# Sample attention with each lot of cache products in one run, zero-padded new values and four cache buffers

## The chip, the core and the metric

The kernel runs on one core of one Trainium2 chip. The metric is the device time of one execution in microseconds (us); a kernel's time is the median over its runs. TensorE is called PE below, VectorE DVE, ScalarE ACT, GpSimd POOL, and SyncE, which issues nearly all DMAs, SP.

## What is computed

The reference is one step of a decoder layer for a prompt of 1024 tokens and for 8 samples of 8 new tokens each. Cut to what matters here, the samples' attention is:

```python
def dilated_group_sample(q, kk, vv, window, dilation):   # kk, vv: cache rows, then the new rows
    idx = (L + jnp.arange(T))[:, None] - dilation * jnp.arange(n_neigh + 1)[None, :]
    kg, vg = kk[:, idx], vv[:, idx]
    s = jnp.einsum('bthd,btjhd->bthj', q, kg) * SCALE
    s = jnp.where(valid[None, :, None, :], s, NEG_INF)
    return softmax_attend(s, vg, 'bthj,btjhd->bthd')
# three (window, dilation) groups, merged by their softmax denominators
```

Around it stand a norm and an input projection with a convolution branch, the prompt's own dilated attention, an output projection, a gated feed-forward block with a short convolution, and a last norm.

## The kernel before, in words

All tokens (1024 of the prompt and 64 of the samples) go through the projections together, as 128-row tiles of features by 1088 tokens. The twelve heads are handled as six pairs p = 0 to 5. `project(p, ...)` makes q, k and v of a pair with three `gemm` calls (lines 184 to 186, three fp32r products each, evicted by DVE at line 447); `sample_attention(p, ...)` is the samples' attention of the pair; `prompt_heads` is the prompt's.

Sample attention runs for p = 0, 1, 2 in a first stage, between the projections (zone "S", from about 99 to 229 us of the profile), and for p = 3, 4, 5 in a second stage, among the prompt's heads and the first part of the output projection (zone "U", from about 395 to 524 us). After that come the rest of the output projection and the feed-forward block, which the change doesn't touch.

In one pair, the 8 samples form four column groups j of 32 rows, and the samples of one group are two halves g = 0, 1. The cache keeps 768 positions, cut in two lots c of 384. So there are four key tiles (g, c) and four value tiles (g, c), each 128 x 1536 numbers (768 KB), which `load_cache` (line 168) brings into a rotation of buffers named "cr": three of them before.

- Scores (line 544): for each lot c, for each g, one key tile is asked for and four products are made, one for each j. Their output is 32 rows high, so that four stand side by side in the array (the profile shows such a product as 128*32). The 64 new keys are one more product in the second lot (line 537, 128*128).
- DVE adds the mask and takes the minimum (line 546), ACT takes the exponential (549), PE turns the weights round in seven transposes (556), the last of which is 64 columns wide, and ACT copies them out in three pieces (558).
- Weighted values (lines 563 and 570): for each g, first the new tokens' values, four products with 64 rows (64*32), then for each c one value tile and 3 x 4 products (128*32). Each fp32 product is two PE instructions in the trace.
- ACT scales the result (572), PE turns it back (575), and DVE puts it in place (582).

The program is written without an order of its own: a framework puts every instruction into its engine's queue by a simulated timeline and by priorities (`tc.high_priority`, `tc.issue_after`), when the kernel is built. Each engine then works through its queue strictly in that order, and an instruction that has to wait holds up what is queued behind it. The products on 32 rows were scheduled one by one, so that other work stands between those of one lot.

Of the kernel before, what the change touches and what calls it, by code (L numbers as in the profile page):

```python
# [20 lines left out]
AF = mybir.ActivationFunctionType  # L21
# [3 lines left out]
P = 128  # L25
D = 1024
S = 1024
B = 8
T = 8
NS = B * T  # L30
# [8 lines left out]
NKEY = NCACHE + NS  # L39
# [7 lines left out]
CH = 384  # L47
NCH = NCACHE // CH
# [32 lines left out]
def trunk_kernel(tc, xT, w_in, w_out, w_gate, w_up, w_down, par, kc, vc, sa, sf, pmask, smask,  # L81
                 yT, kT, vT, ca, cas, cf):
    nc = tc.nc
    with (
# [34 lines left out]
        def zt(z, tag, bufs, s, w=N, dt=F32):  # L119
            return zone[z].tile([P, w], dt, tag=tag, name=nm(s), bufs=bufs)  # L120
# [8 lines left out]
        ident = cp.tile([P, P], F32, name="ident")  # L129
# [295 lines left out]
        def project(p, pump):  # L425
# [39 lines left out]
            def sample_part(c):  # L465
                if c < 2:
                    nc.scalar.activation(new[:, c * NS:(c + 1) * NS], xs[c][:, S:N], AF.Copy,
                                         scale=(1.0 if c else -0.125))
                else:
                    pt = bank(*gbank[0])  # L470
                    nc.tensor.transpose(pt[:NS, :P], xs[c][:, S:N], ident)
                    nc.scalar.activation(vn, pt[:NS, :P], AF.Copy)

            def prompt_part(c):
                x = xs[c]
# [38 lines left out]
        def sample_attention(p, Z, masks):  # L514
            mask, z = masks
            SB, PB = SBUFS[Z][1:]
# [10 lines left out]
                    nc.vector.tensor_copy(zg[g][r, :].rearrange("p (j c) -> p j c", c=32)[:, :, o:o + T],  # L527
                                          src.rearrange("p (j g t) -> p g j t", g=2, t=T)[:, g])
            st = sp.tile([P, 4], F32, tag="sst", name=nm("sst"), bufs=2)
            y = zt(Z, "S", SB, "sy", NKEY)  # L530
            for c in range(NCH):
                ps = bank(Z, "ss", PB)
                n = CH
                first = None
                if c == NCH - 1:
                    n += NS
                    first = nc.tensor.matmul(ps[:, CH:n], za, new[:, NS:], start=True, stop=True)
                for g in range(2):
                    t = load_cache(Z, kc[p, g, c])
                    for j in range(4):  # L540
                        with ExitStack() as order:
                            if first:
                                order.enter_context(tc.issue_after(first.ins))
                            nc.tensor.matmul(ps[32 * j:32 * j + 32, :CH], zg[g][:, 32 * j:32 * j + 32], t[:, j],
                                             start=(g == 0), stop=(g == 1))
# [3 lines left out]
            nc.scalar.activation(y, y, AF.Exp, bias=st[:, 1:2], scale=-1.0, accum_out=st[:, 2:3])  # L549
            nc.vector.reciprocal(st[:, 3:4], st[:, 2:3])  # L550
            pT = zt(Z, "S", SB, "spt", 7 * P)
            for k0, nk in ((0, 4), (4, 3)):
                pt = bank(Z, "ss", PB)
                for k in range(nk):
                    n = min(P, NKEY - (k0 + k) * P)
                    nc.tensor.transpose(pt[:n, k * P:(k + 1) * P], y[:, (k0 + k) * P:(k0 + k) * P + n], ident)
                for (a, e, n) in ([(0, 4, P)] if k0 == 0 else [(0, 2, P), (2, 3, NS)]):
                    nc.scalar.activation(pT[:n, (k0 + a) * P:(k0 + e) * P], pt[:n, a * P:e * P], AF.Copy)
            o2 = zt(Z, "S", SB, "so", 2 * P)
            for g in range(2):  # L560
                po = bank(Z, "ss", PB)
                for j in range(4):
                    nc.tensor.matmul(po[32 * j:32 * j + 32, :P], pT[:NS, 6 * P + 32 * j:6 * P + 32 * j + 32], vn,
                                     start=True, stop=False)
                for c in range(NCH):
                    t = load_cache(Z, vc[p, g, c])
                    for k in range(CH // P):
                        i = CH // P * c + k
                        for j in range(4):
                            nc.tensor.matmul(po[32 * j:32 * j + 32, :P], pT[:, i * P + 32 * j:i * P + 32 * j + 32],  # L570
                                             t[:, j, k * P:(k + 1) * P], start=False, stop=(i == 5))
# [248 lines left out]
        i = 0  # L820
# [818 lines left out]
```

## Time and profile before

| what | value |
|---|---|
| time, median of 3 runs | 1341.75 us (1339.65 to 1345.99) |
| the profiled execution: its own time / span of the profile | 1339.82 us / 1338.0 us |
| PE busy | 97% of the span |
| DVE, ACT, POOL busy | 70%, 42%, 36% |
| mean DMA rate over the span | 157 GB/s |

The profile is one execution. A view of the profile groups instructions by line and tile; the timeline gives start, length and, in brackets, the idle time of the engine ahead of an instruction and what ended it. Matmuls overlap, so their lengths add up to more than the time they take, and what one of them costs PE is read from start to next start.

### The profile page before, as it was taken

To read this page: it belongs to the slowest core of one execution; us is meant where nothing else is said; L and a number is where in the kernel's file an instruction comes from. 1 tells how busy PE (TensorE), PEld (TensorE's weight loads), DVE (VectorE), ACT (ScalarE), POOL (GpSimd) and SP (SyncE) were. 2 spreads that over 40 slices of the span, in tenths; PEclk is the share of its full clock that TensorE was granted. 3 is DMA by queue.
4 is the path that set the end of the run, shared out by engine and by line. 5 is a ranking of instruction groups with operands and counts; after the bars stand their busy time and mean duration, and the time that the engine had idled before them with its cause. 6 is when DMAs were issued, how large, how long until landed. Compare 5 with 4: busy or idle time off the path is not lost.

```text
span 1338.0 us, 25862 instructions
## 1 busy us (share of the span) xinstructions
PE 1297.1 (97%) x10275; PEld 1245.7 (93%) x10275; DVE 937.9 (70%) x1789; ACT 559.8 (42%) x1128; POOL 477.0 (36%) x375
## 2 busy tenths in 40 slices
PE   7999999999999999988999999999999999999996
PEld 7998988999978887888999999999999999999996
DVE  6379779656666657688976676676766669867656
ACT  6312222256674556445633233332333335334432
POOL 1311211211101103430756456564565534444710
PEclk9999999999999999999999999999999999999999
DMA  8147675955689889262033231332213296352412
GB/s 290 56 128 260 234 275 179 242 163 135 206 249 273 270 261 255 90 219 80 2 122 122 91 109 46 122 122 91 99 56 122 76 337 234 108 178 93 156 40 96
DMA packets 92762, 210.27 MB, mean 157 GB/s; under 512 B 13793, under 2 KB 42721, under 8 KB 92641
## 3 DMA queue, kind: packets, MB, share of 16 engines
q1 hardware_dynamic: 92640, 208.62, 48.1%
q8 instruction: 81, 1.33, 0.4%
q14 instruction: 41, 0.33, 0.1%
HBM read 152.55 MB, written 56.04 MB: 156 GB/s over the span
## 4 chain that ended last, share of the span: by engine, by line
PE 56%; DVE 3%; issue 1%; ACT 0%; DMA 0%; DVEq 0%; ACTq 0%
PE g L918 5%; PE g L919 5%; PE g L916 5%; PE py L918 5%; PE py L916 4%; PE py L919 4%; PE px L916 3%; PE pz L918 3%; PE px L919 3%; PE pz L919 3%; PE pz L916 3%; PE px L918 3%; PE g L1490 1%; PE g L1491 1%; PE g L1492 1%; DVE sq L1073 1%
## 5 line engine op out<-in xcount | busy, mean ns | idle before, releaser
L160 POOL TENSOR_TENSOR wl<-wr,wh 128x1024 fp32r<-128x1024 f32 (+1 forms) x36 | 66.9, 1858 | 320.0 <-PE g L186 279.7
L184 PE MATMUL g<-xh,wh 128*128 128x384 f32 (+1 forms) x472 | 158.3, 335 | 0.6 <-DVE qkv L447 0.6
L186 PE MATMUL g<-xh,wl 128*128 128x384 f32 (+1 forms) x472 | 157.1, 333 | 0.0
L185 PE MATMUL g<-xl,wh 128*128 128x384 f32 (+1 forms) x472 | 156.8, 332 | 0.0
L919 PE MATMUL g<-ux,as 128*128 128x272 f32 x504 | 145.1, 288 | 0.0
L918 PE MATMUL g<-ux,as 128*128 128x272 f32 x504 | 144.8, 287 | 0.0
L916 PE MATMUL g<-ux,as 128*128 128x272 f32 x504 | 144.8, 287 | 0.0
L1021 POOL TENSOR_TENSOR wb<-wr,wb 128x512 fp32r<-128x512 f32 x84 | 122.8, 1474 | 49.6 <-ACT wb L1020 49.6
L1373 POOL TENSOR_TENSOR as<-ar,as 128x640 fp32r<-128x640 f32 (+1 forms) x56 | 91.5, 1646 | 100.8 <-ACT as L1372 89.1
L1020 ACT ACTIVATE wb<-wr 128x512 fp32r<-128x512 f32 x84 | 52.5, 629 | 160.7 <-DVE wr L1037 101.8
L692 ACT ACTIVATE y<-y,m 128x128 f32<-128x128 f32 (+1 forms) x192 | 88.7, 467 | 26.9 <-DVE m L680 16.7
L916 PEld LDWEIGHTS g<-ux,as 128*128 128x128 f32 x504 | 95.0, 189 | 0.0
L919 PEld LDWEIGHTS g<-ux,as 128*128 128x128 f32 x504 | 94.8, 188 | 0.0
L918 PEld LDWEIGHTS g<-ux,as 128*128 128x128 f32 x504 | 94.7, 188 | 0.0
L1243 DVE SCALAR_TENSOR_TENSOR fc<-gb,prm,fc 128x1104 f32<-128x1104 f32 x44 | 83.4, 1914 | 14.8 <-ACT fc L1241 14.5
L1021 POOL TENSOR_TENSOR wa<-wr,wa 128x512 fp32r<-128x512 f32 x42 | 57.6, 1375 | 97.5 <-ACT wa L1020 73.6
L184 PEld LDWEIGHTS g<-xh,wh 128*128 128x128 f32 x472 | 89.4, 189 | 3.0 <-issue 1.6
L186 PEld LDWEIGHTS g<-xh,wl 128*128 128x128 f32 x472 | 89.3, 189 | 2.2 <-issue 2.1
L185 PEld LDWEIGHTS g<-xl,wh 128*128 128x128 f32 x472 | 89.5, 190 | 0.6 <-issue 0.2
L655 DVE CUSTOM_DVE_ANT_0 y<-s,pmk 128x128 f32<-128x128 f32 (+1 forms) x192 | 63.5, 379 | 37.0 <-PE s L651 34.5
L397 DVE SCALAR_TENSOR_TENSOR cacc<-gp,prm,cacc 128x1024 f32<-128x1024 f32 x60 | 86.8, 1447 | 0.0
L1463 DVE TENSOR_TENSOR x<-g,x 128x544 f32<-128x544 f32 x76 | 52.5, 717 | 32.9 <-PE g L919 32.9
(370 smaller groups left out, 4244.1 us busy)
## 6 DMA issues: line engine op xcount, KB each, us to landing
cr<-in_kc SPq DMA_DIRECT2D x24, 768.0 KB, 7.9
cr<-in_vc SPq DMA_DIRECT2D x24, 768.0 KB, 6.8
ux<-ub SPq DMA_DIRECT2D x63, 272.0 KB, 4.4
kk<-dk SPq DMA_DIRECT2D x48, 256.0 KB, 6.8
wr<-in_w_gate SPq DMA_DIRECT2D x22, 512.0 KB, 3.3
wr<-in_w_up SPq DMA_DIRECT2D x22, 512.0 KB, 4.4
wr<-in_w_in SPq DMA_DIRECT2D x20, 512.0 KB, 5.5
ub<-u SPq DMA_DIRECT2D x18, 544.0 KB, 4.0
```

The costliest lines, as they stand in the source:

```text
L160: lo_eng.tensor_sub(lo, raw, hi.bitcast(F32))
L184: nc.tensor.matmul(ps[c], whi[:, k, :], xh[:, t0:t0 + n], start=(k == 0), stop=False)
L185: nc.tensor.matmul(ps[c], whi[:, k, :], xl[:, t0:t0 + n], start=False, stop=False)
L186: nc.tensor.matmul(ps[c], wlo[:, k, :], xh[:, t0:t0 + n], start=False, stop=(k == nk - 1))
L397: eng.scalar_tensor_tensor(acc[:, :S], gp[:, j:j + S], col(w0 + j), acc[:, :S], op0=ALU.mult, op1=ALU.add)
L692: nc.scalar.activation(y, y, AF.Exp, bias=m[:, 4 * g + i:4 * g + i + 1], scale=-1.0, accum_out=den[:, g, 2 * hd + u, i:i + 1])
L916: nc.tensor.matmul(ps, whi[:, k, :], xh[:, t], start=(start and k == 0), stop=False, skip_group_check=True)
L918: nc.tensor.matmul(ps, whi[:, k, :], xl[:, t], start=False, stop=False, skip_group_check=True)
L919: nc.tensor.matmul(ps, wlo[:, k, :], xh[:, t], start=False, stop=(k == nk - 1), skip_group_check=True)
L1021: nc.gpsimd.tensor_sub(lo, x, hi.bitcast(F32))
L1243: nc.vector.scalar_tensor_tensor(c[:, :W], gb[i][:, t:t + W], col(C_FW + 3 * f + t), c[:, :W], op0=ALU.mult, op1=ALU.add)
L1373: nc.gpsimd.tensor_sub(lo, raw, hi.bitcast(F32))
```

## The change

The number of cache buffers goes from three to four in both zones. Both tiles that a lot needs are asked for ahead of its products. The products of a lot then carry a high priority and are written in an order in which the tile that was asked for last is used first: for the scores g = 1 and then g = 0; for the values, positions 3, 4, 5, then the new tokens, then 0, 1, 2. The new tokens' values are padded with zero rows from 64 to 128 (a memset of `vn` on POOL), and so are the weights (`y` is 896 wide, with its last 64 columns set to zero on POOL), so that these products have the same shape as the others, the last transpose is full, and ACT copies in two pieces instead of three. The line numbers of the changed kernel differ a little: the scores are line 544 again, the transposes 555, the weighted values 566, the memsets 435 and 532.

```diff
-SBUFS = {"S": (3, 3, 2), "U": (3, 3, 1)}
+SBUFS = {"S": (4, 3, 2), "U": (4, 3, 1)}
...
-            vn = vn[:NS, :]
+            nc.gpsimd.memset(vn[NS:, :], 0.0)
...
-            y = zt(Z, "S", SB, "sy", NKEY)
+            y = zt(Z, "S", SB, "sy", 7 * P)
+            nc.gpsimd.memset(y[:, NKEY:], 0.0)
...
-                for g in range(2):
-                    t = load_cache(Z, kc[p, g, c])
-                    for j in range(4):
-                        with ExitStack() as order:
-                            if first:
-                                order.enter_context(tc.issue_after(first.ins))
-                            nc.tensor.matmul(ps[32 * j:32 * j + 32, :CH], zg[g][:, 32 * j:32 * j + 32], t[:, j],
-                                             start=(g == 0), stop=(g == 1))
+                tiles = [load_cache(Z, kc[p, g, c]) for g in range(2)]
+                with tc.high_priority(offset=AHEAD), tc.issue_after(first.ins) if first else nullcontext():
+                    for g in (1, 0):
+                        for j in range(4):
+                            nc.tensor.matmul(ps[32 * j:32 * j + 32, :CH], zg[g][:, 32 * j:32 * j + 32], tiles[g][:, j],
+                                             start=(g == 1), stop=(g == 0))
...
                 for k in range(nk):
-                    n = min(P, NKEY - (k0 + k) * P)
-                    nc.tensor.transpose(pt[:n, k * P:(k + 1) * P], y[:, (k0 + k) * P:(k0 + k) * P + n], ident)
-                for (a, e, n) in ([(0, 4, P)] if k0 == 0 else [(0, 2, P), (2, 3, NS)]):
-                    nc.scalar.activation(pT[:n, (k0 + a) * P:(k0 + e) * P], pt[:n, a * P:e * P], AF.Copy)
+                    nc.tensor.transpose(pt[:, k * P:(k + 1) * P], y[:, (k0 + k) * P:(k0 + k + 1) * P], ident)
+                nc.scalar.activation(pT[:, k0 * P:(k0 + nk) * P], pt[:, :nk * P], AF.Copy)
...
-                for j in range(4):
-                    nc.tensor.matmul(po[32 * j:32 * j + 32, :P], pT[:NS, 6 * P + 32 * j:6 * P + 32 * j + 32], vn,
-                                     start=True, stop=False)
-                for c in range(NCH):
-                    t = load_cache(Z, vc[p, g, c])
-                    for k in range(CH // P):
-                        i = CH // P * c + k
+                tiles = [load_cache(Z, vc[p, g, c]) for c in range(NCH)]
+                jobs = [(CH // P * c + k, tiles[c][:, :, k * P:(k + 1) * P]) for c in range(NCH) for k in range(CH // P)]
+                jobs.append((6, vn[:, None].to_broadcast([P, 4, P])))
+                with tc.high_priority(offset=AHEAD):
+                    for n, (i, v) in enumerate(jobs[3:] + jobs[:3]):
                         for j in range(4):
                             nc.tensor.matmul(po[32 * j:32 * j + 32, :P], pT[:, i * P + 32 * j:i * P + 32 * j + 32],
-                                             t[:, j, k * P:(k + 1) * P], start=False, stop=(i == 5))
+                                             v[:, j], start=(n == 0), stop=(n == 6))
```

What this does to the order on the engines is seen at three places. The first is PE in stage S, at the weighted values of the first pair. "ss" is the PSUM bank, "cr" a cache tile, "vn" the new tokens' values, "spt" the turned weights, "g" a product of the projection. Before:

```order
L185 MATMUL g_1176<-xl_169,wh_1063 128x384
L186 MATMUL g_1176<-xh_168,wl_1065 128x384
L563 MATMUL ss_978<-vn_619,spt_964 32x128 x4
L570 MATMUL ss_978<-cr_983,spt_964 32x128 x12
L570 MATMUL ss_978<-cr_997,spt_964 32x128 x12
L563 MATMUL ss_1012<-vn_619,spt_964 32x128 x4
L570 MATMUL ss_1012<-cr_1017,spt_964 32x128 x12
L184 MATMUL g_1176<-xh_172,wh_1063 128x384
```

The fourth tile's products (cr_1031) stand 42 rows further down, behind forty projection products and a transpose, in a run of their own. Now, at the same place:

```order
L185 MATMUL g_1133<-xh_132,wh_1058 128x320
L186 MATMUL g_1133<-xl_133,wh_1058 128x320
L566 MATMUL ss_979<-cr_982,spt_966 32x128 x3
L566 MATMUL ss_1013<-cr_1016,spt_966 32x128
L566 MATMUL ss_979<-cr_982,spt_966 32x128
L566 MATMUL ss_1013<-cr_1016,spt_966 32x128
L566 MATMUL ss_979<-cr_982,spt_966 32x128
```

The run goes on like this for 47 more rows: all 56 products of both halves g stand in it, with no projection product between them. As both halves have the same priority, their products alternate, one of bank ss_979 and one of bank ss_1013, the second three behind the first.

The second place is PE in stage U, at the weighted values of the second half of pair p = 3. "s", "t" and "o" are tiles of the prompt's attention. Before:

```order
L563 MATMUL ss_4726<-vn_2001,spt_4678 32x128 x4
L570 MATMUL ss_4726<-cr_4731,spt_4678 32x128
L651 MATMUL s_4233<-kk_3926,qw_3924 128x256
L651 MATMUL s_4233<-kk_3929,qw_3924 128x256
L651 MATMUL s_4233<-kk_3926,qw_3924 128x256
L651 MATMUL s_4233<-kk_3929,qw_3924 128x256
L570 MATMUL ss_4726<-cr_4731,spt_4678 32x128 x6
L719 MATMUL t_4270<-ident,y_4126 128x128
```

Now, with the last projection product ahead and a transpose of the prompt behind:

```order
L186 MATMUL g_6063<-ml_4638,wh_6036 128x320
L187 MATMUL g_6063<-mh_4637,wl_6038 128x320
L566 MATMUL ss_4732<-cr_4735,spt_4685 32x128 x12
L566 MATMUL ss_4732<-vn_2004,spt_4685 32x128 x4
L566 MATMUL ss_4732<-cr_4733,spt_4685 32x128 x12
L752 MATMUL t_4014<-ident,db_4012 128x128 x4
```

What was cut into five runs is one. Not every lot of stage U is whole: at three places an "o" group of the prompt, which has the same priority, still stands inside a values run.

The third place is SP at the start of stage U: "smk" is the mask, "qs" and "kk" are the prompt's queries and keys, "mx" an input of the output projection. Before:

```order
L509 DMA smk_4635<-in_smask 128x832
L168 DMA cr_4648<-in_kc 128x1536
L596 DMA qs_3719<-dq_1997 64x1024 x2
L604 DMA kk_3926<-dk_1998 64x1024 x2
L604 DMA kk_3929<-dk_1998 64x1024 x2
L168 DMA cr_4654<-in_kc 128x1536
L168 DMA cr_4663<-in_kc 128x1536
L268 DMA mx_6268<-mixed_85 128x1088
L168 DMA cr_4669<-in_kc 128x1536
```

Now:

```order
L510 DMA smk_4641<-in_smask 128x832
L169 DMA cr_4655<-in_kc 128x1536
L169 DMA cr_4657<-in_kc 128x1536
L169 DMA cr_4670<-in_kc 128x1536
L169 DMA cr_4672<-in_kc 128x1536
L592 DMA qs_3724<-dq_2000 64x1024 x2
L600 DMA kk_3931<-dk_2001 64x1024 x2
L600 DMA kk_3934<-dk_2001 64x1024 x2
```

All four key tiles of the pair are asked for in a row, ahead of the prompt's queries and keys.

More of the change, by code (lines that the diff above doesn't have):

```diff
@@ L53 @@
 AHEAD = 4000
-SBUFS = {"S": (3, 3, 2), "U": (3, 3, 1)}
+AHEAD = 4000
+SBUFS = {"S": (4, 3, 2), "U": (4, 3, 1)}
 NS1, PN = 3, 4
@@ L471, in sample_part @@
                     nc.tensor.transpose(pt[:NS, :P], xs[c][:, S:N], ident)
-                    nc.scalar.activation(vn, pt[:NS, :P], AF.Copy)
+                    nc.scalar.activation(vn[:NS, :], pt[:NS, :P], AF.Copy)
             def prompt_part(c):
@@ L548, in sample_attention @@
                                                scalar=(st[:, 0:1] if c else 3e38), accum_out=st[:, c:c + 1])
-            nc.scalar.activation(y, y, AF.Exp, bias=st[:, 1:2], scale=-1.0, accum_out=st[:, 2:3])
+            nc.scalar.activation(y[:, :NKEY], y[:, :NKEY], AF.Exp, bias=st[:, 1:2], scale=-1.0, accum_out=st[:, 2:3])
             nc.vector.reciprocal(st[:, 3:4], st[:, 2:3])
```

## The prediction

> **What bounds the kernel now.** I read the page first: the busy times and the chain that ended last.
>
> ```profile
> PE 1297.1 (97%) x10275; PEld 1245.7 (93%) x10275; DVE 937.9 (70%) x1789; ACT 559.8 (42%) x1128; POOL 477.0 (36%) x375
> PE 56%; DVE 3%; issue 1%; ACT 0%; DMA 0%; DVEq 0%; ACTq 0%
> ```
>
> PE is busy 97% of the time and the chain runs over it; nothing else holds more than 3%. So a microsecond that PE saves, or waits less, is one off the end, unless another engine or the DMA queue then comes last. The sums over the two stretches with sample attention say how near those are. The columns are busy time of PE, PEld, DVE, ACT and POOL, then the granted clock, the DMA share and GB/s.
>
> ```profile
> 100.00:230.00 130.00, 125.00 (x1059) 111.71 (x1052) 109.85 (x172) 27.18 (x48) 20.51 (x8) 0.99 0.67 239
> 200.00:222.00 22.00, 22.00 (x205) 19.69 (x203) 22.00 (x33) 4.56 (x8) 3.32 (x1) 1.00 0.59 210
> 382.00:521.00 139.00, 133.74 (x1275) 110.95 (x1273) 87.44 (x360) 84.14 (x257) 14.33 (x14) 1.00 0.90 265
> ```
>
> In stage S PE idles 5.0 of 130 us; DVE has 20 us left over, but none between 200 and 222. In stage U PE idles 5.3 of 139 us and the DMA engines are 90% busy. These are the two limits behind PE.
>
> Next, what PE waits for in the sample products (tile "ss" on PE, then its timeline).
>
> ```profile
>   DMA cr<-in_vc: 5.1, 3
>   DMA cr<-in_kc: 0.6, 1
> 131.89 0.86 PE L570 MATMUL ss<-cr,spt 128*32 128x128 f32 x24 [2.21 <-DMA cr<-in_vc]
> 226.16 1.51 PE L570 MATMUL ss<-cr,spt 128*32 128x128 f32 x24 [2.20 <-DMA cr<-in_vc]
> ```
>
> Cache tiles cost PE 5.7 us of waiting: 4.4 in stage S, both times the fourth value tile, which had no buffer until the first was used up, and 1.3 in stage U.
>
> The products also cost PE something by standing in small runs among products of another shape. The timeline of one run among projection products, and of a double one:
>
> ```profile
> 108.03 0.34 PE L184 MATMUL g<-xh,wh 128*128 128x384 f32 x1
> 108.21 0.34 PE L185 MATMUL g<-xl,wh 128*128 128x384 f32 x1
> 108.47 0.85 PE L544 MATMUL ss<-cr,qz 128*32 128x384 f32 x8
> 109.26 0.44 PE L186 MATMUL g<-xh,wl 128*128 128x384 f32 x1
> 109.54 0.34 PE L184 MATMUL g<-xh,wh 128*128 128x384 f32 x1
> ...
> 99.24 1.50 PE L544 MATMUL ss<-cr,qz 128*32 128x384 f32 x16
> 100.67 0.32 PE L537 MATMUL ss<-new,qz 128*128 128x64 f32 x1
> ```
>
> Projection products start 0.175 us apart. With the eight instructions between them, 108.21 to 109.54 is 1.33 us, 0.98 more than two such steps. Sixteen take 1.43 us from start to next start and eight 0.79, so eight inside a run are worth 0.64. The rest, 0.98 - 0.64 = **0.34 us, is the price of one run**, however long it is. The same for the weighted values:
>
> ```profile
> 119.39 0.34 PE L186 MATMUL g<-xh,wl 128*128 128x384 f32 x1
> 119.66 0.42 PE L563 MATMUL ss<-vn,spt 64*32 64x128 f32 x8
> 120.01 1.52 PE L570 MATMUL ss<-cr,spt 128*32 128x128 f32 x48
> 121.46 0.42 PE L563 MATMUL ss<-vn,spt 64*32 64x128 f32 x8
> 121.81 0.86 PE L570 MATMUL ss<-cr,spt 128*32 128x128 f32 x24
> 122.61 0.45 PE L184 MATMUL g<-xh,wh 128*128 128x384 f32 x1
> 122.89 0.33 PE L185 MATMUL g<-xl,wh 128*128 128x384 f32 x1
> ```
>
> 48 take 1.45 us and 24 take 0.80, so 24 inside a run are worth 0.65, or 0.027 each. From 119.39 to 122.89 are 3.50 us: two projection steps 0.35, 88 instructions 2.38, one run 0.34, and 0.43 left for the three changes between 64 and 128 rows: **0.14 us for each**.
>
> **The change part by part.**
>
> *Runs.* In the timeline of PE such runs are 15 in stage S (the first and the last are quoted: 99.24, 226.16) and 27 in stage U, from the first row below to the last:
>
> ```profile
> 395.46 0.85 PE L544 MATMUL ss<-cr,qz 128*32 128x384 f32 x8
> ...
> 519.55 0.42 PE L563 MATMUL ss<-vn,spt 64*32 64x128 f32 x8
> 519.90 0.86 PE L570 MATMUL ss<-cr,spt 128*32 128x128 f32 x24
> 521.44 0.86 PE L570 MATMUL ss<-cr,spt 128*32 128x128 f32 x24 [0.68 <-DMA cr<-in_vc]
> ```
>
> By the order of the changed kernel they are 3 for each pair in S (two lots, one run of values), 9 in all, and 5 for each pair in U, 15 in all. The row changes go altogether, since padded values have the shape of the others: three for each pair in S, two in U. Stage S: 6 x 0.34 + 9 x 0.14 = 3.3 us. Stage U: 12 x 0.34 + 6 x 0.14 = 4.9 us. The products themselves stay as many. Together **-8.2 us**, all on PE. The seventh transpose, now 128 columns wide, counts nothing, since both widths last the same:
>
> ```profile
> L556 PE MATMUL ss<-ident,sy x42: 270/272/297, 114.6 to 509.8; 128*128 128x128 f32 x36, 128*64 128x128 f32 x6
> ```
>
> *Waits for tiles in S.* With four buffers and the value tiles asked for as soon as a lot of keys is done, the fourth tile's request no longer stands behind the first value tile's use. It is issued after the second scores lot, and the values begin 27 to 32 rows of other products, seven transposes and 21 rows after that: for the first pair about 53 x 0.17 + 0.8 = 9.8 us. Tiles take this long to land:
>
> ```profile
> DMA to landing us min/median/max: 4.2/7.3/11.9
> ```
>
> The median leaves 2.5 us to spare, the slowest is 2.1 us late; I take both waits as gone, **-4.4 us** (bounds: -4.4, and +1.9 if all three pairs wait 2.1 us). What is late next in S is DVE (rival 2).
>
> *The clock after the second wait.*
>
> ```profile
> 132.00:134.00 2.00, 2.00 (x33) 1.80 (x33) 0.00 (x0) 0.37 (x1) 0.00 (x0) 1.00 0.94 335
> 226.00:228.00 2.00, 1.84 (x25) 1.39 (x26) 2.00 (x4) 0.26 (x1) 0.00 (x0) 0.50 0.03 13
> 222.00:224.00 2.00, 1.37 (x8) 0.88 (x6) 2.00 (x5) 0.00 (x0) 0.00 (x0) 1.00 1.00 406
> 227.60 0.64 PE L184 MATMUL g<-xh,wh 128*128 128x320 f32 x1
> 228.57 0.47 PE L184 MATMUL g<-xh,wh 128*128 128x320 f32 x1
> ```
>
> After the wait that ended at 131.89 the granted clock stayed at 1.00; after the one at 226.16, which came on top of 0.6 us of idleness at 222 to 223, it was 0.50. There the 24 instructions took 1.44 us (226.16 to 227.60) instead of 0.80, and the projection products behind them up to 0.27 us a step instead of 0.15, five of them: 0.64 + 0.6 = 1.2 us. With the wait this goes too: **-1.2 us**. The Trainium skill ("TensorE: Matmul & The Clock Gate", Part 1) has the clock halve only after an idle window of about 3.4 us. The trace disagrees, since 2.2 us and 0.6 us sufficed. By the page's threshold neither wait would have cost clock and the sum below would be 1.2 us smaller; it speaks against the change too, as waits gathered ahead of a run get longer each.
>
> *Waits for tiles in U.* The 1.3 us of before are gone by the same argument as in S. New is that the first products of the stage wait for two tiles, not one: before, PE reached the first lot at 395.46 just as its first tile was there, and the second was used later. A tile of 768.0 KB at the stretch's 265 GB/s is 3.0 us. So the first lot comes up to 3.0 us later, and the second, with two more tiles (6.0 us) against a double lot (1.43) and some 1.3 us of other rows, up to 3.3 more. Bounds 0 (other rows were put ahead of the lot) and +6.3; I take one tile, **+3.0**, and -1.3: **+1.7 us**. PE's queue holds prompt products behind this wait.
>
> *The start.* A fourth key tile is now asked for ahead of the last two tiles of x: at the 290 GB/s of the page's first slice 2.7 us later for these. The early products wait for x's split already once:
>
> ```profile
> GB/s 290 56 128 260 234 275 179 242 163 135 206 249 273 270 261 255 90 219 80 2 122 122 91 109 46 122 122 91 99 56 122 76 337 234 108 178 93 156 40 96
> 20.52 0.44 PE L339 MATMUL g<-xl,wh 128*128 128x384 f32 x1 [1.18 <-DVE xl L260]
> ```
>
> There is no wait after that, so the last tiles of x had time; bounds 0 and +2.7, I take **+0.5**.
>
> *Off the path.* Twelve memsets on POOL, by these rows between 0.12 and 0.42 us each, some 3 us of an engine that has 20.51 of 130 us busy:
>
> ```profile
> L511 POOL MEMSET qz<- x2: 416/420/423, 0.9 to 377.1; 128x384 f32 x2
> L358 POOL MEMSET gp<- x2: 124/124/125, 20.5 to 23.6; 128x30 f32 x2
> POOL wl L160 <- PE g L186: 279.7, 26, 22.1
> ```
>
> A memset waits for the last reader of its buffer, and the next weights' low part (wl) is queued behind it. But that one waits for PE itself (26 times, 279.7 us), so the memset's wait lies inside it; if not, a late wl holds up PE's next projection. ACT copies in two pieces instead of three, for which PE never waits here. Both count nothing.
>
> *Sum.* -8.2 - 4.4 - 1.2 + 1.7 + 0.5 = -11.6 us. The profiled execution's own time is 1339.82 us (span 1338.0), 1.9 us under the median of 1341.75, so in terms of the median: 1341.75 - 11.6 = **1330.1 us**. From no change, a measurement here can tell about 0.5%, 6.7 us.
>
> **The rivals.**
>
> 1. *The DMA queue takes stage U's gain back.* For it: 90% busy, and every lot waits for its second tile with all prompt products behind. Against it: four buffers hold two lots, and 10% of 139 us is 14 us. If the four lots of pairs 4 and 5 also wait for one tile of 3.0 us: +12.0, 1342.1 us, no change.
>
> 2. *DVE is the bound of S.* For it: 22.00 of 22.00 us busy at 200 to 222. PE would come to the evictions earlier and wait there. Then what the third pair gains (2.2 + 1.2 + 1.1 = 4.5 us) is lost: 1334.6 us. Against it: 20 us left over in the stage.
>
> 3. *The alternating values lose their overlap.* The trace shows four 32-row products side by side (0.027 us each) only in the order j = 0, 1, 2, 3 of one bank. Now two banks alternate, three products apart, so the groups run 0, 1, 2, 0, 3, 1, 0, 2 and so on. If one that isn't next in line must wait for the one ahead, 112 instructions take the 0.109 us of a lone round (four times 0.027) each, 12.2 us instead of 3.0: +9.2 in each pair of S, 27.5 us in all, 1357.6 us. It makes the kernel slower than no change once fewer than 1.3 run side by side on average. Against it: if each only waits for its own column group, any four neighbours in that sequence after the first few still hold all four groups. The Trainium skill ("TensorE: Matmul & The Clock Gate", Part 3, what overlaps) lets a weight load overlap only where the row group differs, which column groups with the same 128 rows never do. By that rule even before's products could not overlap, and they do: 24 in 0.65 us.
>
> ```profile
> L570 PEld LDWEIGHTS ss<-cr,spt x576: 106/110/177, 120.0 to 521.9; 128*32 128x32 f32 x192
> ```
>
> One load alone takes 0.110 us by this row.
>
> **How the numbers follow.** The forecast 0.64, rival 1 0.18, rival 2 0.12, rival 3 0.06. The forecast is over 0.5% faster except where its unknown terms all come out high; rival 2 lies at the bound (1335.0), half to each side; rival 1 is no change. So faster 0.68, same 0.25, slower 0.07. The range goes down by the terms that may be too careful (the 3.0 and 0.5 us not lost, and as much again from prompt work that fits better): 1322; and up to rival 1: 1342. It leaves out rival 3 and what exceeds rival 1.
>
> **What would show it right or wrong.** Right: 24 runs in PE's timeline instead of 42, no 64*32 rows; no wait over 1 us for a value tile in S and a clock of 1.00 at its end; a wait of about 3 us at the first lot of U; the 112 values instructions of a pair in S in about 3.0 us. Wrong: those 112 in 6 us or more (rival 3); PE waiting for "cr" in most lots of U (rival 1); more PE waits for DVE at "qkv" in S (rival 2).

## The result and the profile after

The changed kernel took 1349.74 us (median of 7 runs, 1348.65 to 1357.0), the kernel before 1342.54 us beside it (7 runs). The ratio is 1.0064, with a 95% interval of 1.0039 to 1.0089: 0.6% slower, where 1330.1 us and faster had been forecast. The profiled execution has a span of 1347.8 us, 9.8 more than before; the medians are 7.2 us apart, as the execution profiled before (1339.82 us) was one of its quicker ones.

The page of the changed kernel, with the two rows that stood first in the prediction:

```profile
PE 1297.3 (96%) x10275; PEld 1253.7 (93%) x10275; DVE 946.9 (70%) x1789; ACT 559.0 (41%) x1122; POOL 475.5 (35%) x387
...
PE 77%; DVE 12%; DMA 6%; issue 2%; ACT 1%; SPq 1%; POOL 1%; DVEq 0%; ACTq 0%
```

PE is as busy as before, but in the chain that ended last DVE has gone from 3% to 12% and DMA from 0% to 6%. The forecast counted both as lying off the path; now they are on it.

The same stretches as before (busy time of PE, PEld, DVE, ACT, POOL, then granted clock, DMA share, GB/s), and one from the end of stage U:

```profile
100.00:230.00 130.00, 125.45 (x1083) 117.00 (x1082) 110.04 (x172) 27.47 (x46) 24.17 (x16) 1.00 0.69 234
200.00:222.00 22.00, 20.20 (x213) 18.92 (x212) 21.92 (x34) 3.87 (x7) 3.59 (x2) 1.00 0.45 127
382.00:521.00 139.00, 128.96 (x1264) 111.26 (x1263) 83.47 (x318) 79.54 (x236) 28.45 (x21) 0.98 0.90 279
570.00:590.00 20.00, 11.32 (x86) 9.55 (x86) 10.29 (x19) 8.00 (x15) 0.00 (x0) 0.77 0.35 117
```

Over S, PE idles 4.6 of 130 us, hardly less than the 5.0 before. From 200 to 222 us DVE is still full (21.92 of 22.00) and now PE is not. In U, PE idles 10.0 us instead of 5.3. At 570 to 590 PE is busy for 11.32 of 20 us at a clock of 0.77: nothing is left to run there.

What the change does to the products came out as forecast. PE's timeline of one run of weighted values:

```profile
113.89 0.31 PE L186 MATMUL g<-xl,wh 128*128 128x320 f32 x1
114.12 1.54 PE L566 MATMUL ss<-cr,spt 128*32 128x128 f32 x48
115.46 0.64 PE L566 MATMUL ss<-vn,spt 128*32 128x128 f32 x16
115.90 1.52 PE L566 MATMUL ss<-cr,spt 128*32 128x128 f32 x48
117.34 0.41 PE L187 MATMUL g<-xh,wl 128*128 128x320 f32 x1
117.59 0.31 PE L185 MATMUL g<-xh,wh 128*128 128x320 f32 x1
```

All 112 products stand together; they take 3.22 us from 114.12 to 117.34. From 113.89 to 117.59 are 3.70 us: 112 x 0.027 = 3.02, two projection steps of 0.15, and 0.38 for the run. There are 24 such runs, 9 and 15, and no 64*32 row. PE waits in S for none of the value tiles. It waits for DVE instead, twice before a lot and once at the stage's end:

```profile
131.29 0.53 PE L544 MATMUL ss<-cr,qz 128*32 128x384 f32 x4 [1.27 <-DVE qz L528]
...
176.36 0.53 PE L544 MATMUL ss<-cr,qz 128*32 128x384 f32 x4 [0.88 <-DVE qz L528]
...
219.03 0.41 PE L185 MATMUL g<-xh,wh 128*128 128x384 f32 x1 [1.80 <-DVE qkv L452]
```

In U the waits of PE from 382 to 530 us (total, times, longest) are led by a load that the prediction gave no price, the queries of a prompt head ("qs"). For cache tiles ("cr") its lots wait only 1.2 us:

```profile
PE s L647 <- DMA qs<-dq: 4.7, 2, 3.7
PE t L715 <- ACT ph L721: 2.3, 1, 2.3
PE ss L544 <- DMA cr<-in_kc: 1.2, 1, 1.2
```

The queries' own view (tile "qs", 382 to 560 us), first in the changed kernel and then before it; the slowest now takes 14.1 us to land, 3.6 more, while the median hardly moves:

```profile
DMA to landing us min/median/max: 5.4/7.5/14.1
```

```profile
DMA to landing us min/median/max: 4.1/7.0/10.5
```

How U begins and ends is seen in the first and last starts (us) of groups of PE. Before: the projections (g from xh, L184), the weighted values of the prompt's heads (L740), the output projection (g from mh, L184), and the first products of the next stage (g from mh, L916):

```profile
L184 PE MATMUL g<-xh,wh x472: 304/335/636, 36.5 to 375.0; 128*128 128x384 f32 x120, 128*128 128x320 f32 x38
...
L740 PE MATMUL o<-ph,vf x288: 272/273/324, 270.4 to 567.6; 128*64 128x128 f32 x144
...
L184 PE MATMUL g<-mh,wh x144: 305/336/442, 389.4 to 578.6; 128*128 128x384 f32 x96, 128*128 128x320 f32 x48
...
L916 PE MATMUL g<-mh,wh x64: 285/288/396, 579.9 to 609.4; 128*128 128x272 f32 x64
```

After, the first three in the same order, and then the timeline of PE's last step of the stage and of the first product of the next:

```profile
L185 PE MATMUL g<-xh,wh x472: 302/335/635, 37.8 to 369.2; 128*128 128x384 f32 x120, 128*128 128x320 f32 x38
...
L736 PE MATMUL o<-ph,vf x288: 272/273/323, 263.7 to 577.3; 128*64 128x128 f32 x144
...
L185 PE MATMUL g<-mh,wh x144: 305/336/522, 387.0 to 569.7; 128*128 128x384 f32 x96, 128*128 128x320 f32 x48
```

```profile
580.45 0.82 PE L752 MATMUL t<-ident,db 128*128 128x128 f32 x4 [2.33 <-DVE db L749]
586.33 1.05 PE L912 MATMUL g<-mh,wh 128*128 128x272 f32 x3 [5.05 <-ACT mh L963]
```

The last projection product starts 5.8 us earlier than before, and the next stage begins 6.4 us late, so 12.2 us are lost in between. The output projection, which can be moved about, ended 8.9 us earlier; the last prompt head, on which the next stage hangs, ended 9.7 us later. PE did the work that was free to move first, and then stood still until the last head had gone through DVE, ACT and a DMA. The remaining 3.4 of the 9.8 us are lost after 1140 us, where PE waits twice for DVE (1.07 us at 1149.73 and 1.40 us at 1155.11); in the kernel before it waits for nothing there.

### The profile page after: what moved, and what is told of

It is laid out like the page before. It is cut to its first block, busy times and chain, and to the rows that moved or that the text cites. A ratio compares the mean times of both kernels' runs of the same rounds, so it can differ in the third digit from the quotient of the medians.

```text
span 1347.8 us, 25877 instructions
## 1 busy us (share of the span) xinstructions
PE 1297.3 (96%) x10275; PEld 1253.7 (93%) x10275; DVE 946.9 (70%) x1789; ACT 559.0 (41%) x1122; POOL 475.5 (35%) x387
## 4 chain that ended last, share of the span: by engine, by line
PE 77%; DVE 12%; DMA 6%; issue 2%; ACT 1%; SPq 1%; POOL 1%; DVEq 0%; ACTq 0%
PE g L185 6%; PE g L186 6%; PE g L187 6%; PE py L914 4%; PE py L912 4%; PE py L915 4%; DVE cacc L398 4%; PE g L912 3%; PE g L915 3%; PE g L914 3%; PE s L647 3%; PE pz L912 3%; PE o L736 3%; PE pz L914 3%; PE px L912 3%; PE px L915 3%
## 5 line engine op out<-in xcount | busy, mean ns | idle before, releaser
L1017 POOL TENSOR_TENSOR wa<-wr,wa 128x512 fp32r<-128x512 f32 x42 | 65.8, 1569 | 158.0 <-ACT wa L1016 115.0
L398 DVE SCALAR_TENSOR_TENSOR cacc<-gp,prm,cacc 128x1024 f32<-128x1024 f32 x60 | 83.5, 1392 | 0.1
L159 ACT ACTIVATE wh<-wr 128x1024 fp32r<-128x1024 f32 (+1 forms) x36 | 29.5, 820 | 125.9 <-PE g L187 86.4
```

Source lines behind the costliest of these rows:

```text
L398: eng.scalar_tensor_tensor(acc[:, :S], gp[:, j:j + S], col(w0 + j), acc[:, :S], op0=ALU.mult, op1=ALU.add)
L1017: nc.gpsimd.tensor_sub(lo, x, hi.bitcast(F32))
```

## The experiments

All ratios are to the kernel before in the same comparison, with 95% intervals.

**One stage each.** The first theory was that S gains and U alone loses. The edit for S; `lots_attention` is the changed code, `tile_attention` the code before, and for U alone the zones are swapped:

```diff
-SBUFS = {"S": (4, 3, 2), "U": (4, 3, 1)}
+SBUFS = {"S": (4, 3, 2), "U": (3, 3, 1)}
+        def sample_attention(p, Z, masks):
+            return (lots_attention if Z == "S" else tile_attention)(p, Z, masks)
```

> The change in stage S alone (lots, padding, four buffers there; stage U as before the change). Theory: what the change saves in S is kept, and the loss lies wholly in U. In the changed kernel the last projection product of stage S/P was 5.9 us earlier than before (375.0 to 369.2 us), so this run should come out about 6 us under the kernel before: 1336 to 1338 us, and faster than the changed kernel by 12 to 14. Rival: the loss comes from the prompt work that S displaces, wherever that ends up; then this run stays at 1345 us or above although U is as before.

> The change in stage U alone (stage S as before). Theory: between 375 and 586 us the changed kernel lost 12.3 us (5.9 ahead at the last projection product, 6.4 behind at the first product of the next stage), all of it from U's own change, so this run should be some 9 to 12 us above the kernel before: 1351 to 1354 us. Rival (the prompt heads displaced by S do it): about 1342 us, as before.

S alone took 1347.93 us, 1.0038 (1.0018 to 1.0058). U alone took 1346.83 us, 1.0023 (0.9997 to 1.0049). The theory fell: S alone loses, although its last projection product started 4.9 us earlier (370.1 instead of 375.0 us).

**Priority and queue in U.** The first edit takes the raised priority from the lots in U (the same condition stands at their scores). The second holds one block of cache tiles behind the queries that PE had waited 3.75 us for:

```diff
-                with tc.high_priority(offset=AHEAD):
+                with tc.high_priority(offset=AHEAD) if Z == "S" else nullcontext():
```

```diff
+                with tc.issue_after(asked[8]) if Z == "U" and p == 4 else nullcontext():
                     tiles = [load_cache(Z, kc[p, g, c]) for g in range(2)]
```

> The changed kernel, with the lots of stage U at their own place in the order of the program: no raised priority there (S keeps it). Theory 1 (the queue): the prompt heads' loads stand behind blocks of cache tiles in the DMA queue, which this leaves as it is at the first pairs; 1346 to 1350 us. Theory 2 (the filler): with raised priority the sample products are spent too early, and nothing is left to run while the last prompt heads go through ACT and DVE (waits of 2.3, 5.1 and 1.3 us at 573 to 586 us); without it these waits shrink by 6 to 8 us: 1341 to 1344 us.

> The changed kernel, with the key tiles of the fifth pair (the second of stage U) asked for only after the query loads of the head that the PE waited 3.75 us for at 433 us. Theory 1 (the queue): that wait goes, the heads behind it come 3 to 6 us earlier, and so does the end of the stage: 1342 to 1346 us. Theory 2 (the filler): the wait goes, but the waits at the end of the stage grow by as much, since the last head's chain through ACT and DVE sets it: 1348 to 1351 us.

Without the priority the kernel took 1351.92 us, 1.0071 (1.0048 to 1.0094), so taking the priority away gains nothing. With the tiles held back it took 1349.55 us, 1.0054 (1.0034 to 1.0073). The one wait went, others came (3.7 us ahead of a head's scores at 509 us), and the next stage began at 584.9.

**Prompt heads first on PE.** If the heads end the stage, let them go first, in the changed kernel and, as a control, in the kernel before (the same edit stands around `finish()`):

```diff
-                    sc = scores(p, hd, u)
+                    with tc.high_priority(offset=2 * AHEAD):
+                        sc = scores(p, hd, u)
```

> The changed kernel, with all steps of the prompt heads (scores, weighted values, norms) at a priority above that of the sample lots and the projections. Theory 3 (the order): the change made the scheduler put projection and sample products ahead of the prompt heads from 337 us on, the last head ends at 577 instead of 568 us, and since only that head's chain is left then, PE waits about 10 us at 573 to 586. With the heads first, the last head should end by 568 us or earlier, the next stage begin by 578, and the time be 1337 to 1342 us. Rival (the heads go as fast as the DMA queue, DVE and ACT let them, whatever PE's order): no gain, 1347 to 1351 us.

> The kernel before with the same raised priority of the prompt heads, as the control: what the change itself is worth where the order of the heads is not left to its side effects. Theory 3: before's heads were not late, so little moves, 1339 to 1345 us, and the changed kernel with heads first is 3 to 8 us faster than this. Rival (the change costs in itself): the changed kernel with heads first is no faster than this.

The changed kernel took 1354.26 us, 1.0059 (1.004 to 1.0078), and the kernel before 1353.65 us, 1.0059 (1.0043 to 1.0076). Theory 3 fell: heads first gain the changed kernel nothing that can be told (1.0064 without), and they cost the kernel before 0.6%. In the changed kernel the heads came some 10 us earlier up to about 400 us and lost that again in U.

**What U's end hangs on.** U without sample attention, once with its 24 tiles still loaded (these two lines in its place), once without them:

```diff
+                            t = load_cache(Z, src[a])
+                            nc.tensor.matmul(ps[:32, :32], z[:, :32], t[:, 0, :32], start=True, stop=True)
```

> The changed kernel without the sample attention of stage U: each of its 24 cache tiles is still loaded and read by one small product, the rest (lots, their evictions, transposes, values) is left out and zeros are written. It frees some 18 us of PE. Theory 3, that the chain of the last prompt head and not PE's amount of work sets the end of the stage: the next stage begins at 575 to 584 us instead of 586.3, hardly sooner. Rival (PE's work is the bound): at 565 to 569 us.

> As the run with tiles only, but without the 24 tiles of stage U either (18.9 MB, some 70 us of the DMA queue at 265 GB/s), and without the rule that holds back the last tiles of x behind them. If the queue paces the prompt heads, their query loads land in 4 us as in the stage before and the next stage begins 10 us or more ahead of the run with tiles only; if not, within 4 us of it.

The second also lets go of a rule that held the last tiles of x behind those cache tiles. One execution each took 1346.91 us and 1328.31 us. The first products of the next stage, with tiles only and with none:

```profile
L928 PE MATMUL g<-mh,wh x64: 282/288/596, 585.0 to 613.7; 128*128 128x272 f32 x64
```

```profile
L921 PE MATMUL g<-mh,wh x64: 285/288/593, 566.3 to 594.6; 128*128 128x272 f32 x64
```

The landing of the heads' queries, with tiles only and with none:

```profile
DMA to landing us min/median/max: 3.7/7.6/15.1
```

```profile
DMA to landing us min/median/max: 3.6/4.3/8.6
```

Here the case turns. Some 18 us of PE's work taken out of U bring its end 1.3 us forward (586.3 to 585.0). The tiles taken out as well bring it 18.7 us further, and queries land in 4.3 us instead of 7.6. With its tiles, U is bound by the DMA queue, in which the prompt heads' loads stand, and what PE does there is worth next to nothing. How much of the 18.7 us belongs to the rule on x's tiles, and how much to the new order of these programs, was not parted.

**Parts of the change, and more query buffers.** Padding alone; four cache buffers alone; four query buffers (and three cache buffers in U) in the changed kernel; four query buffers in the kernel before:

```diff
-            y = zt(Z, "S", SB, "sy", NKEY)
+            y = zt(Z, "S", SB, "sy", 7 * P)
```

```diff
-SBUFS = {"S": (3, 3, 2), "U": (3, 3, 1)}
+SBUFS = {"S": (4, 3, 2), "U": (4, 3, 1)}
```

```diff
-KB, VB, QB, YB, HB, UB, PT = 4, 2, 2, 7, 8, 2, 2
+KB, VB, QB, YB, HB, UB, PT = 4, 2, 4, 7, 8, 2, 2
```

> The kernel before with the padding alone: zero rows under the new tokens' values and weights, the seventh transpose 128 columns wide, two ACT copies in place of three; tiles, order and buffers of sample attention as before. By the price of a row change (0.14 us, 15 of them) it should gain 2.1 us: 1341 to 1343 us. Theory 4: before's order of the instructions is a good draw of the scheduler, and any edit that shifts its clock draws a worse one; then this run comes out 3 to 8 us slower, 1346 to 1351 us, although it adds no work to PE.

> The kernel before with four cache buffers in both stages and nothing else. By the prediction's terms the waits for the fourth value tile of stage S go (4.4 us, and 1.2 of clock): 1337 to 1339 us. Theory 5 (the queue of stage U paces the prompt heads, and a fourth buffer lets more tiles in ahead of their loads): the gain of S is given back in U, 1342 to 1347 us. Theory 4 (any edit draws a worse order): 1346 to 1351 us.

> The changed kernel with three cache buffers in stage U and four query buffers for the prompt heads in place of two, so that a head's queries are asked for one head ahead. Theory 5 (the heads of stage U wait for their queries behind the cache tiles): the heads come 3 to 6 us apart less, the next stage begins at 574 to 580 us instead of 586, and the time is 1338 to 1343 us. Rival (the order of PE, not the loads): 1346 to 1351 us.

> The kernel before with four query buffers for the prompt heads, as the control to the run with four query buffers in the changed kernel. Theory 5: the heads gain here too, 1335 to 1341 us, and the difference between the two says what the change is worth without the wait for queries. Theory 4 (any edit draws a worse order): 1346 to 1351 us.

Padding alone took 1341.71 us, 0.9982 (0.9957 to 1.0006), 2.5 us less where 2.1 had been worked out; no change that can be told for sure, but not slower. The others, in the order above, took 1351.63 (1.0052, 1.0031 to 1.0073), 1351.32 (1.0055, 1.0029 to 1.0081) and 1352.59 us (1.0059, 1.0036 to 1.0082). In the traces the padding leaves the order of PE's other work all but as it was, while the whole change moved some 3,900 of PE's 9,514 instructions (counted in the built programs). So far every edit that kept all of the work and moved much of the order had lost (U alone by less than its interval). Two causes were mixed: what an edit does, and the new order of everything else.

**The order held.** To part them, every instruction outside sample attention was tied to the place on its engine that it had in the kernel before (a table of places, tied by order-only dependences). In the traces of the runs with this table, PE's work outside sample attention stands in the order of the kernel before.

```diff
         trunk_kernel(tc, *args)
+        keep_order(tc)
```

> The change whole, but every instruction that is not of sample attention stands on its engine in the order in which it stood in the kernel before; only sample attention's own instructions find new places. Theory 6 (re-planning): the changed kernel lost because its scheduler re-planned the rest (some 3,900 of 9,514 rows of PE moved), and prompt heads came later; with the old order the gains that the trace showed are kept, 4.4 us in S and 3 to 5 in U, 1332 to 1337 us. Rival (theory 5, the queue of U: blocks of cache tiles ahead of the heads' loads cost as much as the lots gain): S's gain alone at best, 1339 us, or none, 1343 us and above.

> The mirror: the kernel before, with sample attention tile by tile and three buffers, but the rest of the instructions in the order of the changed kernel. Theory 6: the order alone costs what the change lost and more, as none of its gains are there: 1349 to 1356 us. Rival (the order is harmless, the lots and buffers cost): 1341 to 1345 us, as before.

> Four cache buffers alone, in the kernel before (1351.6 us when the scheduler planned it anew), with the order of the rest kept as before. Theory 6: the loss of 7 us goes, and the gain of the waits in S shows, 1337 to 1341 us. Rival (the fourth buffer costs by the queue): it stays at 1347 us or above.

> The change in stage S alone (1347.9 us when planned anew), with the order of the rest kept. Theory 6: the gain of S arrives at the end, 1337 to 1340 us. Rival (S's gain is lost at the border to U, where PE waits for the heads and the first mixed tiles whatever the order): 1342 to 1346 us.

The change whole took 1348.39 us, 1.0036 (1.0015 to 1.0057). The kernel before in the changed kernel's order took 1368.31 us, 1.0179 (1.0147 to 1.0212); that order was made for other tiles, so this shows only that order alone can cost that much. Four buffers alone took 1362.15 us, 1.0128 (1.0099 to 1.0157). S alone took 1342.86 us, 0.9979 (0.9957 to 1.0001), 5 us less than the same code planned anew.

With the order held, one product can be followed from kernel to kernel. Near the end of S, before, and in the change whole:

```profile
231.01 0.34 PE L184 MATMUL g<-xh,wh 128*128 128x384 f32 x1
...
374.51 0.34 PE L184 MATMUL g<-xh,wh 128*128 128x384 f32 x1
```

```profile
219.18 0.42 PE L259 MATMUL g<-xh,wh 128*128 128x320 f32 x1 [2.23 <-DVE qkv L522]
...
222.81 0.34 PE L259 MATMUL g<-xh,wh 128*128 128x384 f32 x1
...
229.52 0.42 PE L259 MATMUL g<-xh,wh 128*128 128x384 f32 x1 [2.31 <-DVE qkv L526]
...
241.64 0.30 PE L726 MATMUL s<-kk,qs 128*128 128x128 f32 x1 [1.98 <-DMA kk<-dk]
...
371.97 0.34 PE L259 MATMUL g<-xh,wh 128*128 128x384 f32 x1
```

The product of 231.01 starts at 222.81: 8.2 us ahead, close to the 8.9 that the prediction's S terms made, although a wait of 2.23 us for DVE already lies before it. Behind it come another for DVE and one for the first head's keys, 4.3 us together, and the granted clock is 0.54 from 242 to 244 us. The product of 374.51 is only 2.5 us ahead, the one at the start of the next stage (579.9) 6.2 us behind, at 586.1. So S gains and hands back; U loses 8.7. Part of that is the clock, which was 1.00 over this stretch before:

```profile
382.00:521.00 139.00, 127.93 (x1242) 111.18 (x1239) 79.42 (x331) 78.59 (x235) 13.47 (x15) 0.95 0.84 256
```

The run with S alone and the order held has the same code for S. Its two followed products:

```profile
223.81 0.34 PE L259 MATMUL g<-xh,wh 128*128 128x384 f32 x1
...
376.38 0.34 PE L259 MATMUL g<-xh,wh 128*128 128x384 f32 x1
```

It is 7.2 us ahead and then 1.9 us behind: behind the first product stand the same waits (2.39 us for DVE, 2.3 us for keys), and the clock is 0.55 from 245 to 250 us. So what S hands back was 5.7 us in one execution and 9.1 in the other, and a difference of a few us between single executions should not be read as an effect.

**The two bounds, one by one.** The cache tiles too at their old places in the queue; and, on top of that, DVE's convolution steps on half of the columns:

```diff
-                 and i.name not in OWN
+                 and (e == 'SP' or i.name not in OWN)
```

```diff
-                eng.scalar_tensor_tensor(acc[:, :S], gp[:, j:j + S], col(w0 + j), acc[:, :S],
+                eng.scalar_tensor_tensor(acc[:, :S // 2], gp[:, j:j + S // 2], col(w0 + j), acc[:, :S // 2],
```

> The change whole, the rest in the old order, and the cache tiles too are asked for at their old places in the queue, so that none of them gets ahead of a prompt head's loads (the fourth buffer only lets a tile at the head of the queue start sooner). Theory 5 (the queue): the waits for queries in U (1.3 and 3.6 us at 421 and 447 with the old order and free loads) fall back to under 0.7 us, U's lots gain 3 to 5 us, and with 2.5 us from S the time is 1335 to 1339 us. Rival (the lots themselves, in front of the prompt products, delay the heads): the heads of U come 5 us or more late again, 1345 to 1349 us.

> The same, with the convolution's steps on DVE over half of the prompt's columns only (half of it is left out), which frees some 12 us of DVE between 200 and 232 us, where it had no idle time. Theory (rival 2 of the prediction: DVE is the bound at the end of S): the waits of PE for qkv there (2.2 and 2.3 us) go, and the 8 us that PE was ahead at 231 us are kept into the next stage, 4 to 6 us more than in the run with full steps. Rival: the waits stay, as something else comes last (the first head's loads, 2.0 us): within 2 us of that run.

With the loads at their old places the kernel took 1350.8 us, 1.0054 (1.0035 to 1.0073). With half of the convolution, which leaves out work, it took 1339.81 us, 0.9971 (0.995 to 0.9992). All engines between 222 and 235 us (DVE is the third), first with full steps and the loads at their old places, then with half of the convolution, and there the followed products:

```profile
222.00:235.00 13.00, 12.88 (x124) 12.13 (x123) 13.00 (x16) 1.57 (x3) 2.94 (x4) 1.00 0.41 152
```

```profile
222.00:235.00 13.00, 13.00 (x76) 12.43 (x75) 8.56 (x16) 2.14 (x4) 4.26 (x6) 1.00 0.91 248
```

```profile
221.59 0.34 PE L260 MATMUL g<-xh,wh 128*128 128x384 f32 x1
...
364.49 0.34 PE L260 MATMUL g<-xh,wh 128*128 128x384 f32 x1
```

With full steps PE waits there for a value tile, for DVE, and for the first head's keys:

```profile
131.54 0.43 PE L646 MATMUL ss<-cr,spt 128*32 128x128 f32 x8 [2.04 <-DMA cr<-in_vc]
...
213.30 0.44 PE L260 MATMUL g<-xh,wh 128*128 128x384 f32 x1 [1.91 <-DVE sst L630]
...
248.60 0.30 PE L727 MATMUL s<-kk,qs 128*128 128x128 f32 x1 [2.14 <-DMA kk<-dk]
```

With DVE at 8.56 of 13 us all three are gone, and the product of 374.51 starts at 364.49, 10.0 us ahead, where it was 2.8 us behind with full steps (377.34). These 12.8 us are more than the 4 to 6 expected. The half steps free DVE from the start on and not only at the end of S: it is busy for 143.18 us of the first 230 instead of 163.55. So DVE bounds S. That the tile and the keys stood in the queue behind results of DVE is argued, not shown.

U is the other half of the answer. PE's waits from 382 to 530 us, with the order held and loads free, with loads at their old places, and with half of the convolution:

```profile
PE s L726 <- DMA qs<-dq: 5.0, 2, 3.6
```

```profile
PE ss L646 <- DMA cr<-in_vc: 8.0, 3, 4.5
PE ss L624 <- DMA cr<-in_kc: 3.0, 1, 3.0
...
PE s L727 <- DMA qs<-dq: 0.8, 1, 0.8
```

```profile
PE ss L646 <- DMA cr<-in_vc: 6.9, 3, 3.1
PE ss L624 <- DMA cr<-in_kc: 3.3, 1, 3.3
```

The queue decides who waits, not whether someone does. With the tiles ahead, the heads wait for queries, 5.0 us. With the tiles at their old places the queries are nearly there (0.8), but lots that need both their tiles wait 11.0 us for them; the next stage starts at 587.0, so U loses 4.3 us there. The run with four query buffers in the changed kernel shows the same: no wait for queries from 382 to 530 us, and 10.0 us for tiles. The last kernel brings 10.0 us into U, its lots wait 10.2 us, the clock is 0.95 from 382 to 521 us, and the next stage starts at 575.5, 4.4 ahead: U takes back more than half. Four buffers without lots, with the order held, are the worst of the first kind: the heads wait 8.0 us for queries.

## Why the prediction was wrong

The step that failed is the first one, "a microsecond that PE saves, or waits less, is one off the end". Its own proviso, unless another engine or the DMA queue comes last, was met in both stages. A PE that is 97% busy was taken for the bound, while the scheduler fills its gaps with work that is free to move: in U the output projection ended 8.9 us earlier and the stage 6.4 us later.

Stage by stage, up to the last projection product the forecast made 8.4 us (3.3 + 4.4 + 1.2 - 0.5) and 5.8 came. In U it made 3.2 (4.9 - 1.7), and 12.2 were lost. Behind U it made nothing, and 3.4 were lost. The split is rough, as the order of the rest differs, but the largest miss is U's: 15.4 us.

- *Runs, -8.2, and waits in S, -4.4 and -1.2.* Right on PE: 24 runs, 0.38 us each, no wait for a value tile, a clock of 1.00 over S, and, with the order held, 8.2 us ahead at the same product. They did not reach the end; in the changed kernel waits for DVE took the place of those for tiles, and PE's idle time over S is 4.6 us instead of 5.0.
- *DVE in S (rival 2, 0.12).* It has the right mechanism. It was seen, 22.00 of 22.00 us, but charged with the third pair's 4.5 us alone. With the order held, the waits and the lower clock behind the third pair took 5.7 of 8.2 us in one execution and 9.1 of 7.2 in the other; in the changed kernel, 5.8 of the 8.4 us were left at the last projection product.
- *Waits in U, +1.7.* Too small and in the wrong place. The prediction gave the first lot 3.0 us of waiting, where it waits 1.2, and the prompt heads a place "behind this wait" on PE. What the heads' own loads behind the tiles in the queue would cost was not asked, although 90% was quoted. Rival 1 (0.18) names the right bound, the queue, but its sign, lots that wait for tiles, did not show in the changed kernel. Its 12.0 us fit the 11.0 and 10.2 us that the lots wait in the two runs with the loads at their old places, which is partly luck.
- *Rivals as alternatives.* Each was set against the forecast alone. They bind in different stages and add up: -11.6 + 12.0 + 4.5 = +4.9 us, 1346.7 us, against 1349.7 measured. That this comes so near is partly luck too, as the parts do not fit as well: 4.5 stands against 2.6 us missed up to the last projection product, 12.0 against 15.4 in U, and nothing against the 3.4 behind it.
- *The start, +0.5.* The last of the 40 early products (L338, now L339) starts at 33.7 instead of 32.4 us, inside the bounds of 0 and 2.7.
- *The clock in U, 0.* It was put at nothing without a reason. From 382 to 521 us it was 0.98 in the changed kernel and 0.95 with the order held, where it was 1.00 before.
- *Memsets and copies, 0.* Right: padding alone is 0.9982.
- *Rival 3.* Refuted: 112 alternating products in 3.22 us. (Its condition, fewer than 1.3 side by side, is where the loss could be told from no change; the forecast's 11.6 us are used up at about 1.8 already.)
- *Not in the prediction:* the new order of the rest. It cost S alone some 5 us (1347.93 against 1342.86 us). Whether the two late waits for DVE are part of it is open: they are not there in the whole change with the order held, but one of 0.69 us stands at the same place (1149.05 us) in S alone with the order held. For the whole change it made no difference that can be told (1349.74 and 1348.39 us); how its parts offset each other there stays open.

No version that does all of the work was found to beat the kernel before by more than the measurement is uncertain: padding alone and S alone in the old order are 0.2% under it, both with intervals that reach 1.

## What to carry to other kernels

Where a scheduler fills an engine's gaps with movable work, its busy share does not make it the bound: find the chain on which the stage's end hangs (here the last prompt head and its loads), and test it by leaving work out of the engine and, separately, transfers out of the queue. Add the prices of rivals that bind in different stages, instead of choosing the likeliest. When an edit makes a scheduler plan the program anew, hold the order of everything else fixed before giving the time to the edit.

## What the runs showed of the hardware

In U, too, the granted clock fell after waits of PE. After one of 3.75 us it was 0.91 between 430 and 450 us, and the twelve products behind the wait took 2.15 us, where sixteen took 1.50 in the kernel before. After one of 2.28 us, at 501.18, it was 0.56 from 502 to 504 us:

```profile
433.49 0.70 PE L647 MATMUL s<-kk,qs 128*128 128x128 f32 x4 [3.75 <-DMA qs<-dq]
434.12 2.15 PE L544 MATMUL ss<-cr,qz 128*32 128x384 f32 x12
```

```profile
502.00:504.00 2.00, 2.00 (x9) 2.00 (x8) 0.29 (x2) 1.39 (x3) 0.00 (x0) 0.56 1.02 407
```

By the Trainium skill ("TensorE: Matmul & The Clock Gate", Part 1) the clock halves after about 3.4 us of idleness. The first wait agrees with that, the second does not, and neither does the wait of 2.04 us at 131.54 with the loads at their old places (0.54 from 132 to 134 us). After the 1.80 us at 219.03 it stayed at 1.00, and so it did after the 2.21 us at 131.89 in the kernel before. So in these traces the length of a single wait does not settle whether the clock falls; where it does, a wait like the 3.75 us costs about a microsecond more than itself.
